# Spreading the cached keys and values of a small decode batch over the projection, gate and prompt-attention stages of a four-layer trunk

## The chip, the cores and the metric

The kernel runs on one core of a Trainium2 chip. The figure of merit is the device time of one execution in microseconds (us). A core has a matrix engine (PE, with its weight loads shown as PEld), a vector engine (DVE), a scalar engine (ACT), a general engine (POOL) and a queue engine (SP). They run their own instruction lists in order and wait for each other by semaphores. DMAs are issued from SP, ACT or POOL.

## The reference

Four layers of a decoder trunk are computed in one launch, for a prompt of 1024 tokens and for a sample group of 8 sequences with 4 new tokens each. The layers are a gated short convolution, an RG-LRU block, differential attention, and the convolution again. Only the attention layer (the third) is touched here. Its parts, cut:

```python
def diff_attn_project(u, w_in, pos):
    q, k, v, z = jnp.split(u @ w_in, [QK_WIDTH, 2 * QK_WIDTH, 2 * QK_WIDTH + V_WIDTH], axis=-1)
    q = rope_partial(q.reshape(bsz, t, 2 * N_HEADS, HEAD_DIM), pos) * (HEAD_DIM ** -0.5)
    k = rope_partial(k.reshape(bsz, t, 2 * N_HEADS, HEAD_DIM), pos)
...
def diff_attn_prompt(q, k, v, lam):            # per block of 128 queries, causal
        sc = jnp.einsum('bqhd,bkhd->bhqk', qi, k).astype(jnp.float32)
        w = diff_combine(jax.nn.softmax(sc, axis=-1), lam)      # p[head, 0] - lam * p[head, 1]
        return jnp.einsum('bhqk,bkhd->bqhd', w, v)
...
def diff_attn_sample(q, k_new, v_new, cache_k, cache_v, page_table, lam):
    k_past = cache_k[page_table].reshape(bsz, -1, 2 * N_HEADS, HEAD_DIM)
    v_past = cache_v[page_table].reshape(bsz, -1, N_HEADS, V_HEAD_DIM)
    ...                                        # softmax over 2048 past and 4 new keys, then w @ v
def diff_attn_output(o, z, subln_g, lam_init, w_out):
    return (rms_norm(o) * subln_g * (1.0 - lam_init) * jax.nn.silu(z)) @ w_out
```

D_MODEL is 1024, there are 8 heads with two score maps each, a page holds 128 positions, and each of the 8 sequences has 16 pages of past keys and 16 of past values, 512 KB each. So 67 MB of keys and 67 MB of values are read.

## The kernel before

All work is float32; the larger products split an operand into a high and a low part (type float32r) and add the partial products. The attention layer has three stages for the prompt, and PE works through them in this order:

- **Projections** (`qkv`): 48 tiles (q, k and v in two halves each, 8 token tiles each), `qk<n>_<t>`, 24 matmuls each. Tiles of q and k are rotated on DVE, transposed on PE (`qkf`) and stored to DRAM.
- **Gate path** (`zpath`): 8 heads by 3 chunks, `zz<h>_<c>`, 24 matmuls each; tanh on ACT, product on DVE, stored to DRAM (`zd`) and read back in the next stage.
- **Heads** (`heads`): 8 heads by 8 query blocks: scores (`S`), row minima on DVE, exponentials on ACT (`P`), the difference of the two maps on DVE (line 1284), transposition on PE (`wtp`), copy on ACT, product with the values (`pv`). Keys and queries of a head come from DRAM (`kd`, `qd`) into tiles `tok` and are split into the high and low parts `ks` and `qhl`.

Two streams of work for the sample group are threaded into these stages. **Sample keys**: for each sequence and each of two feature halves, 16 half pages (`kp`, 256 KB each, issued from POOL, six buffers) are transposed on DVE into one tile `kt` with a single buffer (line 1476), and 64 groups of small matmuls (`sps`, line 1420, each shown as two records) multiply them by the queries. The document calls these sixteen pieces *halves* and the matmuls of one half a *burst*. After the second half come softmax, `spn` (new keys) and `spt` (transposition), and a store to DRAM (`psd`). **Sample values**: 128 whole pages (`vp`, issued from SP) are multiplied by these weights (`sacc`, line 1524). Keys hold a PSUM area that the values need in part, so all keys come before any value.

How much of a stream stands beside which stage is set by `merge`: as the prompt's stage yields pieces of nominal cost, a debt grows, and the side stream is written out until the debt is paid. The shares are in `self.shares` and `self.ahead`; `rest` writes out what is left. Before, the shares 0.76 and 0.26 put the keys beside the projections and the gate path, and all values stand beside the heads. A scheduler then moves instructions by its own model, mostly within a small distance; the order on each engine is fixed when the program is built.

The tiles `raw` (two buffers) take the raw weights of the gate path and the tiles `tok`. The tiles `zt` of the gate path have two buffers, and each is free again when its store has landed.

## Time and profile before

| what | us |
|---|---|
| median of 3 runs (lowest, highest) | 2407.51 (2405.63, 2414.55) |
| the profiled execution's own time | 2409.33 |
| its span, first to last instruction | 2407.7 |
| projections, 948 to 1350 | 402 |
| gate path, 1350 to 1486 | 136 |
| heads and values, 1486 to 1850 | 364 |

The three stages are 902 us of the span; the layers before and after them are not touched. The stage borders are where the first `qk`, `zz` and `S` matmul start and where the output projection takes over. "Busy" is the time in which an engine had an instruction under way. PE's matmuls overlap, so that an isolated group of them shows a longer busy time than the same group in a dense run.

### The profile page before, as it was taken

Reading aid. Unit: us, or ns where it says so; the run is one execution under the profiler, and the core shown is the slowest. Engines: PE = TensorE matmul, PEld = TensorE weight load, DVE = VectorE, ACT = ScalarE, POOL = GpSimd, SP = SyncE. Lnnn points to the kernel's source line nnn. Section 1 sums busy time; section 2 is a strip of 40 time slices with the busy share of each in tenths; the row PEclk is TensorE's granted clock in tenths of the full one; section 3 lists DMA queues with packets and bytes.
Section 4 is the critical chain, followed back from the end, with each engine's and each line's share of the span. In section 5 each row is a group of like instructions: output and inputs, shape, how many; then the busy total and the mean of one; then the engine's idle time right before and its main releaser. Section 6 shows DMA issues by size and latency. Waiting matters only on the chain.

```text
span 2407.7 us, 45325 instructions
## 1 busy us (share of the span) xinstructions
PE 2277.3 (95%) x17288; PEld 1946.8 (81%) x17288; DVE 1453.2 (60%) x3015; ACT 929.2 (39%) x1906; POOL 337.1 (14%) x541
## 2 busy tenths in 40 slices
PE   7999999999999999988999998888888999999997
PEld 4989999997888886766666886555557999999997
DVE  6865655457456545656555554677675477666555
ACT  4333333346544423322221113667665243333410
POOL 0200000001001000233223322333220000000000
PEclk9999999999999999999999998999999999999999
DMA  9243344423444535768677766999993222222442
GB/s 329 77 145 111 91 121 150 133 82 120 139 131 124 154 108 171 217 201 255 222 242 253 244 189 203 277 298 291 281 299 116 84 85 62 68 59 70 128 131 76
DMA packets 289391, 393.41 MB, mean 163 GB/s; under 512 B 18749, under 2 KB 197054, under 8 KB 289174
## 3 DMA queue, kind: packets, MB, share of 16 engines
q1 hardware_dynamic: 247190, 306.61, 42.1%
q0 software_dynamic: 20480, 67.13, 9.1%
q10 hardware_dynamic: 21504, 16.78, 2.1%
q8 instruction: 136, 2.23, 0.4%
q14 instruction: 81, 0.66, 0.1%
HBM read 331.14 MB, written 59.31 MB: 162 GB/s over the span
## 4 chain that ended last, share of the span: by engine, by line
PE 64%; issue 13%; DMA 11%; POOLq 5%; POOL 2%; DVE 2%; ACT 1%; SPq 1%; DVEq 0%; ACTq 0%
PE op L127 15%; PE inX L612 12%; PE inZ L612 6%; DMA vp<-cache_v 6%; PE xb L127 4%; PE z L127 4%; POOLq L1381 4%; PE in L127 3%; PE inY L612 3%; PE ada L200 3%; PE in L733 2%; PE in L648 2%; PE g L903 2%; POOL kp L1388 2%; PE sacc L1524 1%
## 5 line engine op out<-in xcount | busy, mean ns | idle before, releaser
L1099 PE MATMUL qk<-wq,ua 128*128 128x512 f32 x1152 | 284.1, 401 | 8.7 <-DVE wq L1067 5.5
L1099 PEld LDWEIGHTS qk<-wq,ua 128*128 128x128 f32 x1152 | 213.2, 189 | 68.4 <-DVE wq L1067 8.1
L1476 DVE STREAM_TRANSPOSE kt<-kp 128x512 f32<-128x512 f32 x256 | 172.0, 697 | 138.5 <-DMA kp<-cache_k 107.1
L1388 POOL DMA_DIRECT2D kp<-cache_k x256 | 137.9, 539 | 336.1 <-DVE kt L1476 188.8
L294 DVE SCALAR_TENSOR_TENSOR r<-op,gate,xr 128x384 f32<-128x384 f32 (+1 forms) x96 | 54.2, 570 | 127.4 <-PE op L127 82.5
L1262 ACT ACTIVATE P<-S,rr 128x512 f32<-128x512 f32 (+2 forms) x192 | 110.8, 583 | 47.1 <-DVE rr L1250 31.5
L1210 PE MATMUL S<-ks,qhl 128*128 128x512 f32 (+2 forms) x384 | 110.8, 395 | 13.8 <-ACT P L1262 7.4
L127 PE MATMUL zz<-ua,wz 128*128 128x384 f32 (+1 forms) x576 | 99.0, 331 | 7.0 <-DVE zt L1165 7.0
L1210 PEld LDWEIGHTS S<-ks,qhl 128*128 128x128 f32 x384 | 60.8, 196 | 54.8 <-ACT P L1262 30.7
L127 PEld LDWEIGHTS zz<-ua,wz 128*128 128x128 f32 x576 | 95.6, 193 | 11.4 <-DVE zt L1165 7.8
L127 PEld LDWEIGHTS z<-ub,wrz 128*128 128x128 f32 x576 | 92.6, 188 | 11.7 <-issue 10.1
L1524 PE MATMUL sacc<-vp,pv 128*16 128x256 f32 x1024 | 80.3, 389 | 22.9 <-DMA vp<-cache_v 22.7
L127 PE MATMUL z<-ub,wrz 128*128 128x384 f32 (+1 forms) x576 | 98.2, 326 | 0.0
L1303 PEld LDWEIGHTS pv<-V,wt 128*128 128x128 f32 x576 | 73.7, 194 | 22.5 <-ACT wt L1295 13.4
L127 PEld LDWEIGHTS xb<-ub,wrx 128*128 128x128 f32 x504 | 80.9, 188 | 12.7 <-issue 9.2
L1420 PE MATMUL sps<-kt,qbd 32*32 32x512 f32 x2048 | 78.8, 621 | 11.9 <-DVE kt L1476 11.9
L331 POOL TENSOR_TENSOR rs<-mv,mhalf 128x1 f32<-128x1 f32 (+1 forms) x36 | 19.1, 541 | 504.3 <-DVE mv L329 497.6
L127 PE MATMUL op<-ua,ub 128*128 128x384 f32 (+1 forms) x504 | 89.7, 333 | 0.0
L127 PEld LDWEIGHTS op<-ua,ub 128*128 128x128 f32 x504 | 81.9, 192 | 9.1 <-issue 9.0
L127 PE MATMUL xb<-ub,wrx 128*128 128x384 f32 (+1 forms) x504 | 87.9, 328 | 0.0
L1303 PE MATMUL pv<-V,wt 128*128 128x128 f32 x576 | 82.3, 284 | 5.8 <-ACT wt L1295 5.3
L200 PE MATMUL ada<-wada,ct 128*32 128x512 f32 x384 | 82.7, 616 | 4.1 <-DMA wada<-w_ada 2.9
(492 smaller groups left out, 5112.4 us busy)
## 6 DMA issues: line engine op xcount, KB each, us to landing
kp<-cache_k POOLq DMA_DIRECT2D x256, 256.0 KB, 3.8
vp<-cache_v SPq DMA_DIRECT2D x128, 512.0 KB, 10.0
wada<-w_ada SPq DMA_DIRECT2D x96, 512.0 KB, 4.2
xa<-xat SPq DMA_DIRECT2D x64, 192.0 KB, 2.6
wra<-a_w_in SPq DMA_DIRECT2D x24, 512.0 KB, 4.1
wrb<-a_w_in SPq DMA_DIRECT2D x24, 512.0 KB, 4.1
xr<-xa SPq DMA_DIRECT2D x64, 192.0 KB, 2.5
tok<-kd SPq DMA_DIRECT2D x32, 256.0 KB, 7.0
```

The source lines that it names most:

```text
L127: nc.tensor.matmul(ps[:, :n], wt[:, wp, k], self.ucols(units[k], up, c), start=i == 0, stop=i == 3 * KB - 1)
L200: nc.tensor.matmul(ps[c : c + 32, :], self.ct[:, k], wts[k // 2][:, k % 2], start=k < 4, stop=k >= 4, tile_position=(0, c),)
L612: nc.tensor.matmul(B[tgt][jj][:, :QH], w[n][:, wp, k], mov[k](jj, up), start=new and m == 0, stop=m == 11, skip_group_check=not new)
L1099: nc.tensor.matmul(ps, u[k][:, c0 : c0 + 128], wq[n, k // 2][:, wp, k % 2], start=i == 0, stop=i == 3 * KB - 1)
L1210: nc.tensor.matmul(st[:, o : o + w], qs[h, g][:, part, s, 128 * qj : 128 * qj + 128], ks[h][:, s, l0 : l0 + w], start=part == 0, stop=part ...
L1262: nc.scalar.activation(p[:, o : o + w], x["S"][s][i][:, :w], AF.Exp, scale=-1.0, bias=rr[:, 6 + s : 7 + s], accum_out=rr[:, c : c + 1])
L1303: nc.tensor.matmul(x["pv"], x["w"][kb // 4][:, j : j + 128], V[h][:, kb], start=kb == 0, stop=kb == qb)
L1381: ld, (r,) = nc.values_load_multi_w_load_instructions(self.ptab[0:1, idx : idx + 1], engines=[et], min_val=0, max_val=159)
L1388: d = eng.dma_start(t, a[src].rearrange(pat)[bass.ds(r, 1), :, cs].rearrange("a p f -> p (a f)"))
L1420: nc.tensor.matmul(ps[b][32 * g : 32 * g + 32, r], qf[rows, f, g, k], kt[rows, g, k], start=f == 0 and k == 0, stop=f == 1 and k == 3, til ...
L1476: nc.vector.transpose(ktv[:, :, j], ring.pop(0).rearrange("p (f t) -> p f t", t=32))
L1524: nc.tensor.matmul(acc[32 * g : 32 * g + 16, :], pt[:k, j, g], vv[:k, :, g], start=j == 0, stop=j == NPG, tile_position=(0, 32 * g))
```

## The change

The merging shares become 0.98 and 0.4 (the latter over two chunks of the gate path only, then the rest of the keys is written out), so that all keys stand beside the projections and the first gate chunks. The sample values begin right after, at 0.3 of their nominal cost over the gate path, and the remaining 0.7 beside the heads; their pages get seven buffers instead of five. The stores of the gate path move from SP's queue to ACT's, one chunk late: the store of a chunk is issued behind the tanh of the next. Keys and queries of the prompt heads are fetched once, 256 KB by one DMA where two DMAs of 256 KB each were, with 128 partitions of 512 instead of 128 of 2 by 512; the copies to the other half of the partitions are made on the core. For keys, ACT makes two copies of 64x512 instead of one of 128x1024, and POOL subtracts as before, two times 64x512. For queries, ACT makes two copies of 64x512, DVE two further copies of 64x512 (new), and POOL four subtractions of 64x512 instead of one of 128x1024. Lines behind the edits move by up to 8.

```diff
--- before.py
+++ after.py
@@ -1150,6 +1150,7 @@
             return self.load_w(wv[:, :, c : c + 128], f"wz{h}")
 
         wt = ld(0)
+        late = []
         for h in range(KB):
             nxt = ld(h + 1) if h < KB - 1 else None
             for c in range(3):
@@ -1158,14 +1159,17 @@
                 ps = self.gemm_chunk(wt, u, c, f"zz{h}_{c}")
                 t = self.sm(f"zt{h}_{c}")
                 nc.scalar.activation(t[:, :n], ps[:, :n], AF.Tanh, scale=0.5)
+                if late:
+                    nc.scalar.dma_start(*late.pop())
                 if npr < n:
                     nc.vector.scalar_tensor_tensor(
                         self.szs[:, h], t[:, npr:n], 1.0, ps[:, npr:n], ALU.add, ALU.mult
                     )
                 nc.vector.scalar_tensor_tensor(t[:, :npr], t[:, :npr], 1.0, ps[:, :npr], ALU.add, ALU.mult)
-                nc.sync.dma_start(self.zd[h][:, c0 : c0 + npr], t[:, :npr])
+                late.append((self.zd[h][:, c0 : c0 + npr], t[:, :npr]))
                 yield 10.2 * n
             wt = nxt
+        nc.scalar.dma_start(*late.pop())
 
 
     def heads(self, y):
@@ -1176,11 +1180,10 @@
         ks, V, sz, qs, O, ss = {}, {}, {}, {}, {}, {}
 
 
-        def twice(q, h, g):
-            t = self.raw([128, 2, 512], f"tok{q}{h}_{g}")
-            src = self.qkT[q][128 * h : 128 * h + 128, 512 * g : 512 * g + 512]
-            for rows in halves[0]:
-                nc.sync.dma_start(t[rows], src.rearrange("(s p) f -> p s f", p=64))
+
+        def fetch(q, h, g):
+            t = self.raw([128, 512], f"tok{q}{h}_{g}")
+            nc.sync.dma_start(t, self.qkT[q][128 * h : 128 * h + 128, 512 * g : 512 * g + 512])
             return t
 
         def keys(h, g):
@@ -1190,18 +1193,22 @@
                 nc.sync.dma_start(
                     V[h], self.vd[:, 128 * h : 128 * h + 128].rearrange("(j p) f -> p j f", p=128)
                 )
-            t = twice(1, h, g)
+            t = fetch(1, h, g)
             cs = slice(512 * g, 512 * g + 512)
-            nc.scalar.copy(ks[h][:, :, cs], t)
             for s, (own, oth) in enumerate(halves):
-                lo = ks[h][oth, s, cs]
-                nc.gpsimd.tensor_tensor(lo, t[oth, s], lo.bitcast(F32), ALU.subtract)
+                hi = ks[h][own, s, cs]
+                nc.scalar.copy(hi, t[own])
+                nc.gpsimd.tensor_tensor(ks[h][oth, s, cs], t[own], hi.bitcast(F32), ALU.subtract)
 
         def queries(h, g):
-            t = twice(0, h, g)
+            t = fetch(0, h, g)
             qhl = self.wtile([128, 2, 2, 512], F32R, f"qhl{h}_{g}")
-            nc.scalar.copy(qhl[:, 0], t)
-            nc.gpsimd.tensor_tensor(qhl[:, 1], t, qhl.bitcast(F32)[:, 0], ALU.subtract)
+            for s, (own, oth) in enumerate(halves):
+                hi = qhl[own, 0, s]
+                nc.scalar.copy(hi, t[own])
+                nc.vector.tensor_copy(qhl[oth, 0, s], t[own])
+                for rows in (own, oth):
+                    nc.gpsimd.tensor_tensor(qhl[rows, 1, s], t[own], hi.bitcast(F32), ALU.subtract)
             qs[h, g] = qhl
 
         def product(st, h, qb, s, o, l0, w):
@@ -1589,18 +1596,19 @@
         cq.__exit__(None, None, None)
         ct, self.tmp = self.pool("tmpq", reuse_waits="tile")
         z, ztot = self.zpath(u), 8 * 10.2 * NT
-        merge(itertools.islice(z, 20), ztot, keys, self.shares[1] * KEY_COST)
-
+        merge(itertools.islice(z, 2), ztot, keys, self.shares[1] * KEY_COST)
+        rest(keys)
+
+        self.deal(tp="QU", tps="P", mm="R")
+        values = self.sample_values(u)
+        next(values)
+        merge(itertools.islice(z, 18), ztot, values, self.zshare * VALUE_COST)
         cpa, self.ppa = self.pool("ppa", reuse_waits="tile")
         hs = self.heads(u)
         next(hs)
-        merge(z, ztot, keys, self.shares[1] * KEY_COST)
-        rest(keys)
+        merge(z, ztot, values, self.zshare * VALUE_COST)
         ca, self.pp = self.pool("pp", reuse_waits="tile")
-        self.deal(tp="QU", tps="P", mm="R")
         tot = 64 * 9 * 110.0 + 288 * 324.0 + 16 * 430
-        values = self.sample_values(u)
-        next(values)
 
         def main():
             while True:
@@ -1610,7 +1618,7 @@
                     break
                 yield c
 
-        merge(main(), tot, values, VALUE_COST * self.ahead)
+        merge(main(), tot, values, VALUE_COST * (1 - self.zshare) * self.ahead)
         rest(values)
         ca.__exit__(None, None, None)
         cpa.__exit__(None, None, None)
@@ -1730,7 +1738,7 @@
                 cm.__exit__(None, None, None)
             self.bufs = dict(sm=2)
             self.n_sz, self.n_ks, self.n_p, self.n_tok, self.n_wt, self.n_o = 1, 2, 4, 2, 3, 2
-            self.shares, self.ahead, self.n_vp = (0.76, 0.26), 1.1, 5
+            self.shares, self.zshare, self.ahead, self.n_vp = (0.98, 0.4), 0.3, 1.1, 7
             cc, cp = self.pool("acst", reuse_waits="tile", side="right")
             cr, self.ropep = self.pool("ropep", reuse_waits="tile", side="right")
             self.attn_consts(cp)
```

On PE, in the projections: the burst of sequence 4's second half in the list before (`kt4_1` is its transposed key tile, `qk4_6` the seventh tile of the first half of the v projection):

```order
L1099 MATMUL qk4_6_14554<-wq4_3_13379,ua6_84 128x512 x3
L1099 MATMUL qk4_6_14554<-wq4_3_13379,ua7_85 128x512 x3
L1420 MATMUL sps4_14179<-kt4_1_14278,qbd_9885 32x512 x64
L1429 MATMUL spn4_14647<-ksb_8495,qbd_9885 32x32 x32
L1099 MATMUL qk4_7_14691<-wq4_0_12890,ua0_78 128x512 x3
```

The same burst in the list of the change:

```order
L1099 MATMUL qk4_0_14636<-wq4_3_14010,ua7_85 128x512
L1436 MATMUL spn4_14365<-ksb_8495,qbd_9885 32x32 x6
L1427 MATMUL sps4_13892<-kt4_1_13957,qbd_9885 32x512 x64
L1436 MATMUL spn4_14365<-ksb_8495,qbd_9885 32x32 x26
L1099 MATMUL qk4_0_14636<-wq4_3_14010,ua7_85 128x512 x2
```

It stands some six projection tiles earlier. The last burst (sequence 7, second half) stood behind `zz6_1` and now stands behind `zz0_0`, with 23 gate chunks still to come.

On PE, in the gate path, at the end of chunk `zz1_2` in the list before:

```order
L127 MATMUL zz1_2_16149<-ua6_84,wz1_15715 128x288 x3
L127 MATMUL zz1_2_16149<-ua7_85,wz1_15715 128x288 x3
L127 MATMUL zz2_0_16249<-ua0_78,wz2_15981 128x384 x3
L127 MATMUL zz2_0_16249<-ua1_79,wz2_15981 128x384 x3
L127 MATMUL zz2_0_16249<-ua2_80,wz2_15981 128x384 x3
```

The same place in the list of the change (`vp0_1` is sequence 0's second page of values):

```order
L127 MATMUL zz1_2_17058<-ua6_84,wz1_16719 128x288 x3
L1531 MATMUL sacc0_16898<-vp0_0_16899,pv0_16862 16x256 x4
L127 MATMUL zz1_2_17058<-ua7_85,wz1_16719 128x288 x3
L127 MATMUL zz2_0_17109<-ua0_78,wz2_16931 128x384 x3
L127 MATMUL zz2_0_17109<-ua1_79,wz2_16931 128x384 x3
L127 MATMUL zz2_0_17109<-ua2_80,wz2_16931 128x384 x3
L1531 MATMUL sacc0_16898<-vp0_1_16915,pv0_16862 16x256 x4
```

From here to the end of the gate path stand the products of 32 cached pages and of the new tokens of sequences 0 and 1, 34 in all, where before there was none; before, the first of them stood among the heads.

On DVE, in the heads, around the difference of the two maps of head 0, block 3 (line 1284 before, 1291 after; `rr` holds the row sums) in the list before:

```order
L1281 RECIPROCAL rr0_3_17696<-rr0_3_17696 128x2
L1282 SCALAR_TENSOR_TENSOR rr0_3_17696<-rr0_3_17696,nlam_5858 128x1
L1284 SCALAR_TENSOR_TENSOR P0_3_0_17704<-P0_3_1_17755,rr0_3_17696,P0_3_0_17704 128x512
L1248 TENSOR_REDUCE rr0_4_17757<-S0_4_1_0_17772 128x1
L1250 ISA S0_4_1_1_17776,rr0_4_17757<-S0_4_1_1_17776,cmask_17569,rr0_4_17757 128x128
```

The same place in the list of the change:

```order
L1288 RECIPROCAL rr0_3_18268<-rr0_3_18268 128x2
L1209 CAST qhl1_0_18544<-tok01_0_18542 64x512 x2
L1289 SCALAR_TENSOR_TENSOR rr0_3_18268<-rr0_3_18268,nlam_5858 128x1
L1291 SCALAR_TENSOR_TENSOR P0_3_0_18276<-P0_3_1_18311,rr0_3_18268,P0_3_0_18276 128x512
L1255 TENSOR_REDUCE rr0_4_18313<-S0_4_1_0_18328 128x1
```

The two new copies of the queries of head 1 (they wait for the DMA that brings `tok`) stand in DVE's list in the middle of the softmax of a block of head 0.

## Rows read from the trace of the kernel before

**Rows 1.** The page, part 1: busy us (share of the span) xinstructions.
```profile
PE 2277.3 (95%) x17288; PEld 1946.8 (81%) x17288; DVE 1453.2 (60%) x3015; ACT 929.2 (39%) x1906; POOL 337.1 (14%) x541
```

**Rows 2.** Stages by windows: length, busy us by engine, clock, DMA share, GB/s.
```profile
core 0: us, PE busy (x) PEld busy (x) DVE busy (x) ACT busy (x) POOL busy (x), PEclk, DMA share, GB/s
948.00:1350.00 402.00, 375.12 (x3349) 270.37 (x3350) 221.92 (x459) 97.10 (x152) 112.52 (x209) 0.98 0.73 229
1350.00:1486.00 136.00, 124.58 (x1270) 112.51 (x1270) 67.91 (x125) 27.81 (x46) 38.87 (x62) 0.95 0.63 192
1486.00:1850.00 364.00, 306.55 (x2472) 201.59 (x2471) 255.59 (x661) 240.90 (x732) 102.87 (x73) 0.97 0.93 267
```

**Rows 3.** The chain that ended last, 1530 to 1790, by line.
```profile
by line: DMA vp<-cache_v 50.2%; DMA tok<-qd 8.3%; PE sacc L1524 8.0%; PE S L1210 6.5%; PE pv L1303 5.3%; issue 2.9%; DMA tok<-kd 2.7%; PE wtp L1293 2.6%; DVE os L1530 2.1%; DVE P L1284 1.8%; ACT P L1262 1.4%; DVE rr L1282 1.3%; SPq L1388 1.
```

**Rows 4.** PE's waits, 1490 to 1820: us in total, times, longest.
```profile
PE sacc L1524 <- DMA vp<-cache_v: 22.7, 27, 1.9
PE wtp L1293 <- DVE P L1284: 7.5, 8, 1.8
```

**Rows 5.** Timeline of POOL from 1258, two successive page issues: start us, us.
```profile
1259.77 0.54 POOL L1388 DMA_DIRECT2D kp<-cache_k  x1 [14.60 <-DVE kt L1476]
1261.13 0.54 POOL L1388 DMA_DIRECT2D kp<-cache_k  x1 [0.82 <-DVE kt L1476]
```

**Rows 6.** Timeline of DVE over the same half: start us, us, count, idle before.
```profile
1258.66 3.67 DVE L1476 STREAM_TRANSPOSE kt<-kp 128x512 f32<-128x512 f32 x6 [8.97 <-PE sps L1420]
1262.77 0.71 DVE L1476 STREAM_TRANSPOSE kt<-kp 128x512 f32<-128x512 f32 x1 [0.44 <-DMA kp<-cache_k]
...
1276.55 0.71 DVE L1476 STREAM_TRANSPOSE kt<-kp 128x512 f32<-128x512 f32 x1 [0.76 <-DMA kp<-cache_k]
1281.82 2.29 DVE L1434 TENSOR_REDUCE smx<-sps 128x1 f32<-128x2048 f32 x1 [4.55 <-PE sps L1420]
```

**Rows 7.** Timeline of PE, the burst of the same half.
```profile
1277.32 4.03 PE L1420 MATMUL sps<-kt,qbd 32*32 32x512 f32 x114 [0.81 <-DVE kt L1476]
```

**Rows 8.** Line 1476 in 983 to 1145.5: min/median/max ns, first and last start.
```profile
L1476 DVE STREAM_TRANSPOSE kt<-kp x96: 668/711/715, 983.9 to 1144.4; 128x512 f32<-128x512 f32 x96
```

**Rows 9.** Groups of 948 to 1350: busy us, mean ns, idle before.
```profile
L1476 DVE STREAM_TRANSPOSE kt<-kp 128x512 f32<-128x512 f32 x201 | 135.1, 698 | 107.6 <-DMA kp<-cache_k 78.1 <-PE sps L1420 28.9
L1420 PE MATMUL sps<-kt,qbd 32*32 32x512 f32 x1536 | 61.0, 629 | 11.9 <-DVE kt L1476 11.9
```

**Rows 10.** Groups of 1350 to 1486, PE.
```profile
L127 PE MATMUL zz<-ua,wz 128*128 128x384 f32 (+1 forms) x576 | 99.0, 331 | 7.0 <-DVE zt L1165 7.0
L1420 PE MATMUL sps<-kt,qbd 32*32 32x512 f32 x512 | 17.8, 597 | 0.0
L1451 PE MATMUL spt<-ident,sc 128*128 128x128 f32 x48 | 7.5, 324 | 4.4 <-ACT sc L1439 4.4
```

**Rows 11.** Waits of ACT, 1350 to 1486.
```profile
ACT zt L1160 <- DMA zd<-zt: 37.9, 6, 11.5
```

**Rows 12.** The group of the value products, 1486 to 1850.
```profile
L1524 PE MATMUL sacc<-vp,pv 128*16 128x256 f32 x1024 | 80.3, 389 | 22.9 <-DMA vp<-cache_v 22.7
```

**Rows 13.** DMAs of 1486 to 1850: packets; issues by line, KB, us to landing.
```profile
DMA packets 41675, 97.18 MB, mean 267 GB/s; under 512 B 4032, under 2 KB 15168, under 8 KB 41635
vp<-cache_v SPq DMA_DIRECT2D x128, 512.0 KB, 10.0
tok<-qd SPq DMA_DIRECT2D x28, 256.0 KB, 11.5
tok<-kd SPq DMA_DIRECT2D x25, 256.0 KB, 7.4
```

**Rows 14.** Two windows of 30 us in the heads, columns as in rows 2.
```profile
1610.00:1640.00 30.00, 27.15 (x246) 17.55 (x238) 24.20 (x64) 21.09 (x65) 10.27 (x8) 1.00 0.99 299
1790.00:1820.00 30.00, 28.36 (x260) 17.87 (x260) 24.14 (x70) 21.23 (x71) 4.49 (x5) 1.00 0.69 238
```

**Rows 15.** Line 1284 in the third head (first row) and the last.
```profile
L1284 DVE SCALAR_TENSOR_TENSOR P<-P,rr,P x8: 343/810/1284, 1582.6 to 1621.3; 128x128 f32<-128x128 f32 x1, 128x256 f32<-128x256 f32 x1, 128x384 f32<-128x384 f32 x1, 128x512 f32<-128x512 f32 x1
L1284 DVE SCALAR_TENSOR_TENSOR P<-P,rr,P x8: 354/818/1279, 1796.5 to 1835.7; 128x128 f32<-128x128 f32 x1, 128x256 f32<-128x256 f32 x1, 128x384 f32<-128x384 f32 x1, 128x512 f32<-128x512 f32 x1
```

**Rows 16.** Two DVE lines, whole run: min/median/max ns, first and last start.
```profile
L1282 DVE SCALAR_TENSOR_TENSOR rr<-rr,nlam x64: 199/220/2152, 1493.8 to 1835.3; 128x1 f32<-128x1 f32 x64
L1455 DVE COPY sc<-spt x8: 1184/1222/1225, 1063.9 to 1481.0; 128x1024 f32<-128x1024 f32 x8
```

**Rows 17.** Groups of 1486 to 1850: DVE, then POOL.
```profile
L1282 DVE SCALAR_TENSOR_TENSOR rr<-rr,nlam 128x1 f32<-128x1 f32 x64 | 23.1, 362 | 2.2
...
L1204 POOL TENSOR_TENSOR qhl<-tok,qhl 128x1024 fp32r<-128x1024 f32 x15 | 35.7, 2380 | 114.4 <-ACT qhl L1203 90.3 <-DMA vp<-cache_v 19.8 <-PE pv L1303 4.2
L1198 POOL TENSOR_TENSOR ks<-tok,ks 64x512 fp32r<-64x512 f32 x26 | 34.0, 1309 | 41.4 <-ACT ks L1195 39.9
```

## The prediction

> **What bounds the kernel now.** Over the whole span PE is busy for 95% [rows 1], which says little: the three stages of the attention layer have different limits, so I read the windows of the stages first [rows 2], then the chain of waits inside a stage, then the groups and timelines that give unit prices. In the projections and the gate path PE idles for 27 and 11 us of 402 and 136. In the heads it idles for 57 of 364 us, and there the DMA share is 0.93 over the stage and 0.99 inside it [rows 2, 14]. The chain that ended last shows what the heads wait for: half of it is the transfer of value pages and another 11% the transfers of keys and queries [rows 3]. So the heads are bound by DMA: 97.18 MB in 364 us [rows 13], at a share that leaves no room. PE itself shows only 22.7 us of waits for pages [rows 4], because PE, DVE and ACT go on with queued blocks.
>
> The second thing to see is how the sample keys run. While the tile `kt` has one buffer, a half is a serial loop: transpose 16 half pages, burst, transpose again. POOL issues a page every 1261.13 - 1259.77 = 1.36 us [rows 5]. In the half shown, DVE does six waiting pages at once and then waits for POOL's pages one by one, from 1258.66 to 1276.55 + 0.71 = 1277.26, that is 18.6 us [rows 6]. The burst starts 0.06 us later [rows 7] and is over at 1281.8, when the reduction starts: 4.5 us. After every second half the reduction of 2.29 us stands ahead of the next transposition [rows 6]. That is (2 x 23.2 + 2.3) / 2 = 24.3 us a half as the floor, whatever PE does.
>
> **The change part by part.** All sums are against the profiled execution (2409.33 us; span 2407.7), which lies 1.8 us above the median of 2407.51.
>
> *Keys into the projections.* Before, 201 of 256 half pages were transposed by 1350, with 12 of 16 bursts [rows 9]. Now 15 bursts lie in the projections and the last behind the first gate chunk. PE's own work up to there is 375.1 us of before [rows 2], four more bursts of 4.5, a gate chunk of 99.0 / 24 = 4.1 [rows 10] and some 6 for softmax and transposition of two more sequences: 403 us. With the 15 us of idle time that have nothing to do with keys (27 less 11.9 [rows 9]) PE would be there at 948 + 418 = 1366. But the loop of keys starts at 983.9 [rows 8] and has 16 halves. At the floor it ends at 983.9 + 16 x 24.3 = 1373. From the first 96 pages, six halves that ran nearly without slack, the pace is (1144.4 - 983.9 - 18) / 5 = 28.5 [rows 8], which would give 1440; there several bursts had pieces of projection tiles between their matmuls. In the new order only about one burst in four is broken in that way, so I take a value nearer to the floor, 25.9: the last burst ends at 983.9 + 16 x 25.9 = 1398. PE then stalls before most bursts, two or three us each, 32 us beyond what it must do. I found no cover for this: the list has nothing else for PE to do at these places but what stands behind the burst.
>
> *Gate path.* After the last burst 23 chunks remain, 23 x 4.1 = 95 us. To this come 3 us for the last sequence's softmax and 34 value products (32 pages and two groups of new tokens). A product is 80.3 / 128 = 0.63 us of busy time [rows 12]; in dense work it will be a little less, say 0.6: 20 us. The gate stores on ACT's queue take away the waits that show as 37.9 us on ACT [rows 11] and 7.0 on PE [rows 10], which I have left out above; so I put no stall here. The pages need 17 MB in about 98 us, with 8 MB of weights, stores and reads beside them: 255 GB/s, below the 299 seen [rows 14], so the transfers keep up, without much to spare. The gate path ends at 1398 + 118 = 1516, against 1486.
>
> *Heads.* 32 of the 128 pages are gone, and two are as good as there (17.8 MB), and of the 53 fetches of keys and queries, 256 KB each, half (7 MB) [rows 13]: 97.2 - 17.8 - 7 = 72 MB, at the 299 GB/s of the full window [rows 14] 242 us. DMA no longer binds. What binds next is not shown by any row directly, so I bound it from both sides. *PE*: 306.6 us busy less 34 x 0.6 = 286; where pages had nearly run out, 1790 to 1820, PE was busy for 28.36 of 30 us [rows 14]. 286 / 0.945 = 303, and about 12 for the first fill and the drain: 315. *DVE*: 255.6 us busy [rows 2], and the change adds to it. The 30 copies of 64x512 in this stage have no row; the nearest is 128x1024 in 1.22 us [rows 16], so 0.6 each, 18 us. In that same late window DVE was busy for 24.14 of 30 us, 0.805. Line 1282, which works on one column, takes 0.22 us at the median and 2.15 at most [rows 16], 362 ns on the mean over 64 [rows 17]: it is held up while POOL subtracts. That is 9 us on this line alone, some 20 with the larger lines beside it, against 86 us of POOL's data work. For queries POOL will need 4 x 1.31 instead of 2.38 us [rows 17], 43 us more in the stage, so some 10 us more of such holds. (255.6 + 18 + 10) / 0.805 = 352. Between 315 and 352 I take 335. The last head speaks against the low end: its transfers had already thinned out (a share of 0.69 [rows 14]), yet its eight blocks took 39.2 us from first to last, as against 38.7 in a head amid full DMA [rows 15].
>
> The Trainium skill bears on these holds (page "SBUF — State Buffer", section "Who interferes with whom"): a VectorE instruction with two SBUF inputs contends with a GpSimd instruction that reads SBUF, and whichever starts first holds the port for its whole length. The maxima of line 1282 agree in size, up to one subtraction of 2.38 us. The same section has float32 copies from SBUF to SBUF hold that port too; by it each new copy could also wait for a subtraction that is under way, which is the fourth case below.
>
> *The rest.* ACT makes two copies of 64x512 where one of 128x1024 was, the same number of elements one after the other, and issues the gate stores; I cost both at nothing, since ACT is busy for 27.8 of 136 and 240.9 of 364 us [rows 2]. If ACT is held up by a store that waits for DVE, a tanh is late by that much, with three PSUM banks of slack on PE.
>
> Sum: 1398 + 118 + 335 = 1851, against 1850. The 57 us that the heads had idle are partly won (29 us), and lost again where the keys are pressed into a stage that is too short for their loop (48 us later at the end of the keys' part, of which 18 us come back in the gate path). The forecast is no change that can be measured: 2409.33 + 1 = 2410 us. A measurement of this kernel can tell about 0.5%, 12 us, from no change.
>
> **The rivals.**
> *The heads follow PE.* If the blocks keep PE at 0.945 once pages are no longer late, the heads take 315 us: 1398 + 118 + 315 = 1831, 19 us faster, 2390. For it: the waits for pages are half of the chain [rows 3]. Against it: the last head [rows 15].
> *The keys' loop at its measured pace.* If halves take 28.5 instead of 25.9 us, the last burst ends at 1440 and all behind it is 42 us later: 2452. It decides from about 26.7 us a half (13 us later than I take). For it: that is what the first six halves did; against it: the half at 1258 ran at the floor [rows 6].
> *That the keys keep up*: at 24.3 us a half PE is the limit (1373) and the rest as above: 25 us earlier, 2385. It needs every half at its floor and I give it little.
> *DVE is held by POOL in the heads.* The two copies stand in the middle of the softmax of a block and wait there for the DMA of `tok`, with the difference of the maps queued behind them, and for POOL. At 352 us for the heads the sum is 1868, 18 us slower: 2427. It decides from about 347. For it: the holds already there [rows 16, 17]; against it: DVE is not on the chain for more than some 5% now [rows 3].
>
> **How the numbers follow.** No change 0.40; heads follow PE 0.24; keys keep up 0.08; keys' loop slower 0.12; DVE held 0.16. So faster by over 0.5% 0.32, within 0.5% 0.40, slower 0.28. Within the first case the time lies between 2398 and 2422. The range over cases reaches from 2376, where the heads follow PE and the keys are somewhat better than 25.9, to 2444, where DVE is held and the halves take 27: that leaves out about 2 in 10.
>
> **What would show it.** Right, if the last `sps` burst ends near 1398, with PE waits of `sps` for DVE `kt` at 30 to 50 us in the projections instead of 11.9; if the gate path ends near 1516 with no wait for `zt`; if the heads show a DMA share near 0.75, hardly a PE wait for `vp`, and last some 335 us. Wrong, if halves are 24 or 28 us apart; if `sacc` waits for pages in the gate path by more than 8 us, where I put none; if the two DVE copies of queries cost more than 0.6 us each or leave DVE waiting for `tok`; or if the heads fall below 315.

## The result, and the profile of the changed kernel

The changed kernel takes 2475.73 us (median of 4 runs, 2473.4 to 2481.08) against 2406.57 for the kernel before: a ratio of 1.028, with a 95% interval of 1.0244 to 1.0316. The forecast was no change, 2410 us in 2376 to 2444; the result lies outside, on the slow side. The profiled execution took 2481.08 us, its span is 2479.4 against 2407.7, so 71.7 us are to be found.

Part 1 of its page, as [rows 1]:

```profile
PE 2310.8 (93%) x17288; PEld 1964.6 (79%) x17288; DVE 1485.1 (60%) x3047; ACT 935.8 (38%) x1938; POOL 390.7 (16%) x589
```

PE's busy time grew by 33.5 us with the same 17288 instructions. So part of the loss is PE instructions that show longer, not only waits. The stages as windows, cut at the end of the last burst and of the gate path's matmuls, as the forecast counts them (the first gate chunk lies in the first window):

```profile
core 0: us, PE busy (x) PEld busy (x) DVE busy (x) ACT busy (x) POOL busy (x), PEclk, DMA share, GB/s
948.00:1440.00 492.00, 419.00 (x4048) 297.58 (x4047) 266.62 (x540) 102.72 (x162) 143.09 (x261) 0.93 0.72 223
1440.00:1555.00 115.00, 115.00 (x862) 95.59 (x854) 28.66 (x59) 23.21 (x40) 13.01 (x13) 1.00 0.78 268
1555.00:1920.00 365.00, 303.20 (x2192) 207.83 (x2192) 280.58 (x678) 246.63 (x760) 151.69 (x119) 0.92 0.54 182
```

The keys' part ends at 1440 where 1398 was forecast, the gate path takes 115 us (forecast 118), and the heads 365 (forecast 335). The first and the third are the miss: 42 + 30 us, less 3. The granted clock is 0.93 in the first window and 0.92 in the last, against 0.98 and 0.97 in [rows 2].

**The keys.** PE's longest wait from 948 to 1440 (us in total, times, longest), and the group of the bursts (busy us, mean ns, idle before):

```profile
PE sps L1427 <- DVE kt L1483: 28.3, 7, 7.1
```

```profile
L1427 PE MATMUL sps<-kt,qbd 32*32 32x512 f32 x2048 | 90.2, 734 | 45.1 <-DVE kt L1483 28.3 <-DVE qbd L1420 12.8 <-DVE sc L1463 2.0
```

The first row is the stall that the forecast wanted, 28.3 us where [rows 9] have 11.9; it is just under the 30 to 50 that were named. But bursts also waited for `qbd` (the queries) and for softmax work (`sc`) on DVE, 45.1 us with these. In all PE was idle for 73.0 of the 492 us, 26 more than the 47 (15 + 32) of the forecast, and busy for 419.0, 16 more than its 403: these are the 42 us. What makes work longer can be seen behind a stall. The last half on DVE (start, us, count, idle before it):

```profile
1411.95 3.68 DVE L1483 STREAM_TRANSPOSE kt<-kp 128x512 f32<-128x512 f32 x6 [4.64 <-PE sps L1427]
...
1428.61 0.71 DVE L1483 STREAM_TRANSPOSE kt<-kp 128x512 f32<-128x512 f32 x1 [2.25 <-DMA kp<-cache_k]
1430.88 0.71 DVE L1483 STREAM_TRANSPOSE kt<-kp 128x512 f32<-128x512 f32 x1 [1.56 <-DMA kp<-cache_k]
1433.23 0.71 DVE L1483 STREAM_TRANSPOSE kt<-kp 128x512 f32<-128x512 f32 x1 [1.64 <-DMA kp<-cache_k]
```

The burst behind it on PE:

```profile
1407.46 4.45 PE L1427 MATMUL sps<-kt,qbd 32*32 32x512 f32 x128 [2.41 <-DVE kt L1483]
...
1426.25 0.64 PE L1436 MATMUL spn<-ksb,qbd 32*32 32x32 f32 x50
1434.00 6.07 PE L1427 MATMUL sps<-kt,qbd 32*32 32x512 f32 x128 [7.11 <-DVE kt L1483]
```

Transposing took 22.0 us here (1411.95 to 1433.94; 18.6 in [rows 6]): the last three pages came 2.3 us apart, not 1.36. And the burst took 6.07 us where the one before it took 4.45. The clock around the two bursts, with the columns of the windows above:

```profile
1407.00:1412.20 5.20, 4.74 (x130) 2.50 (x131) 0.56 (x2) 0.00 (x0) 1.80 (x4) 1.00 0.99 340
1426.90:1430.60 3.70, 0.00 (x0) 0.00 (x0) 0.71 (x1) 0.00 (x0) 0.39 (x1) 1.00 0.99 293
1430.60:1434.00 3.40, 0.00 (x1) 0.01 (x1) 1.48 (x3) 0.00 (x0) 0.00 (x0) 0.50 1.10 309
1434.00:1437.40 3.40, 3.40 (x64) 1.21 (x65) 0.38 (x1) 0.00 (x0) 0.00 (x0) 0.50 0.20 70
1437.40:1440.00 2.60, 2.60 (x94) 1.84 (x77) 0.00 (x0) 0.00 (x0) 0.00 (x0) 0.99 0.02 6
```

PE had nothing to do from 1426.9 to 1434.0. In the second half of that pause the granted clock falls to 0.50, that is 1.2 of 2.4 GHz, and the burst's first 64 matmul records run at it for 3.4 us; its last 94 records, some of them the small `spn` matmuls, take 2.6 us at 0.99. Over all 16 halves the means are: transposition 19.8 us, burst 6.1, 2.4 between them, 28.3 together (986.7 to 1440.1). In [rows 6] and [rows 7] transposition and burst are 18.6 and 4.5. The excess of the bursts, 27 us in all, has two parts. Seven bursts stand behind a pause of 3 us or more, with only `spn` or a single projection matmul beside their own; they take 6.0 to 6.2 us, at a clock of 0.68 to 0.72 (11 us). Four have transpositions of projection tiles (`qkf`) between their matmuls; they take 6.1 to 10.2 us, at 0.79 to 0.83, and in the longest PE stands still for 3.65 us (15 us). The other five take 4.5 to 5.4. POOL's pages still start 1.35 us apart in the undisturbed stretch:

```profile
1415.80 0.56 POOL L1395 DMA_DIRECT2D kp<-cache_k  x1 [0.82 <-DVE kt L1483]
1417.15 0.55 POOL L1395 DMA_DIRECT2D kp<-cache_k  x1 [0.79 <-DVE kt L1483]
```

**The gate path.** Groups of PE, 1440 to 1556 (busy us, mean ns, idle before):

```profile
L127 PE MATMUL zz<-ua,wz 128*128 128x384 f32 (+1 forms) x552 | 96.9, 328 | 0.0
L1531 PE MATMUL sacc<-vp,pv 128*16 128x256 f32 x262 | 19.9, 383 | 0.0
```

PE is busy for all 115.0 us of this window. The 7.0 us that `zz` waited for `zt` in [rows 10] are gone, and nothing waits for value pages.

**The heads.** The two windows of [rows 14] again; they lie in the second and the sixth head now:

```profile
1610.00:1640.00 30.00, 27.72 (x245) 16.82 (x241) 23.72 (x54) 22.01 (x65) 13.13 (x12) 1.00 0.86 300
1790.00:1820.00 30.00, 24.71 (x117) 20.12 (x117) 23.21 (x66) 21.36 (x70) 12.06 (x10) 0.73 0.17 54
```

The DMA share is 0.86 and 0.17, in the mean over the stage 0.54 against 0.93. PE did not get busier for it: 24.71 of 30 us with hardly a transfer, at a clock of 0.73. Such a stretch has no value products, since these are all done 158 us before the stage ends (minimum, median, maximum ns; first and last start):

```profile
L1531 PE MATMUL sacc<-vp,pv x1024: 379/379/634, 1460.8 to 1760.9; 128*16 128x256 f32 x171
```

The chain of waits over a stretch of the heads like that of [rows 3]:

```profile
by line: PE S L1217 20.2%; PE pv L1310 13.6%; PE sacc L1531 11.8%; ACT P L1269 9.7%; PE wtp L1300 6.3%; DVE P L1291 5.8%; DVE S L1257 4.0%; issue 3.7%; DVE qhl L1209 2.9%; DVE rr L1289 2.3%; ACT qhl L1208 2.2%; DVE ua L1239 2.2%; ACT wt L13
```

The transfers of values, half of the chain before, are gone from it. In their place stand the pieces of a block's own softmax: scores `S`, exponentials and difference `P`, transposition, products `pv`. The waits of PE, 1560 to 1900, say the same (in [rows 4] the pages headed the list):

```profile
PE S L1217 <- ACT P L1269: 19.9, 29, 2.6
PE pv L1310 <- ACT wt L1302: 18.4, 19, 1.8
...
PE sacc L1531 <- DMA vp<-cache_v: 0.3, 1, 0.3
```

ACT's largest wait in the heads, first of the kernel before, then of the changed one; its releaser is the reduction of row minima on DVE:

```profile
ACT P L1262 <- DVE rr L1250: 31.5, 27, 3.8
```

```profile
ACT P L1269 <- DVE rr L1257: 52.9, 35, 5.0
```

And two DVE groups of that stage, to be set against 924 ns of busy time for the difference before (59.1 us for 64), and 0.6 us estimated for a copy:

```profile
L1291 DVE SCALAR_TENSOR_TENSOR P<-P,rr,P 128x128 f32<-128x128 f32 (+3 forms) x64 | 68.5, 1070 | 2.1
...
L1209 DVE CAST qhl<-tok 64x512 fp32r<-64x512 f32 x30 | 23.3, 776 | 1.1 <-PE S L1217 0.5
```

### The profile page after: what moved, and what is told of

Read it like the earlier page. It is cut to its first block, busy times and chain, and to the rows that moved or that the text cites. A ratio compares the mean times of both kernels' runs of the same rounds, so it can differ in the third digit from the quotient of the medians.

```text
span 2479.4 us, 45392 instructions
## 1 busy us (share of the span) xinstructions
PE 2310.8 (93%) x17288; PEld 1964.6 (79%) x17288; DVE 1485.1 (60%) x3047; ACT 935.8 (38%) x1938; POOL 390.7 (16%) x589
## 4 chain that ended last, share of the span: by engine, by line
PE 69%; issue 13%; POOLq 5%; DVE 4%; DMA 4%; ACT 3%; POOL 2%; SPq 0%; DVEq 0%; ACTq 0%
PE op L127 15%; PE inX L612 11%; PE inZ L612 6%; POOLq L1388 4%; PE xb L127 4%; PE zz L127 4%; PE z L127 4%; PE in L127 3%; PE inY L612 3%; PE S L1217 3%; PE ada L200 3%; PE sacc L1531 2%; PE in L733 2%; PE in L648 2%; PE g L903 2%
## 5 line engine op out<-in xcount | busy, mean ns | idle before, releaser
L1217 PE MATMUL S<-ks,qhl 128*128 128x512 f32 (+2 forms) x384 | 117.7, 416 | 20.5 <-ACT P L1269 19.9
L1269 ACT ACTIVATE P<-S,rr 128x512 f32<-128x512 f32 (+2 forms) x192 | 110.7, 581 | 63.7 <-DVE rr L1257 52.9
L1427 PE MATMUL sps<-kt,qbd 32*32 32x512 f32 x2048 | 90.2, 734 | 45.1 <-DVE kt L1483 28.3
L1427 PEld LDWEIGHTS sps<-kt,qbd 32*32 32x32 f32 x2048 | 36.9, 114 | 82.9 <-issue 34.3
L127 PEld LDWEIGHTS z<-ub,wrz 128*128 128x128 f32 x576 | 92.6, 188 | 11.7 <-issue 10.1
L1211 POOL TENSOR_TENSOR qhl<-tok,qhl 64x512 fp32r<-64x512 f32 x64 | 86.2, 1347 | 93.7 <-ACT qhl L1208 90.6
L667 POOL COPY psv<-cp 128x32 f32<-128x32 f32 x14 | 7.3, 523 | 520.5 <-DVE cp L678 482.5
```

Source lines behind the costliest of these rows:

```text
L127: nc.tensor.matmul(ps[:, :n], wt[:, wp, k], self.ucols(units[k], up, c), start=i == 0, stop=i == 3 * KB - 1)
L1211: nc.gpsimd.tensor_tensor(qhl[rows, 1, s], t[own], hi.bitcast(F32), ALU.subtract)
L1217: nc.tensor.matmul(st[:, o : o + w], qs[h, g][:, part, s, 128 * qj : 128 * qj + 128], ks[h][:, s, l0 : l0 + w], start=part == 0, stop=part ...
L1269: nc.scalar.activation(p[:, o : o + w], x["S"][s][i][:, :w], AF.Exp, scale=-1.0, bias=rr[:, 6 + s : 7 + s], accum_out=rr[:, c : c + 1])
L1427: nc.tensor.matmul(ps[b][32 * g : 32 * g + 32, r], qf[rows, f, g, k], kt[rows, g, k], start=f == 0 and k == 0, stop=f == 1 and k == 3, til ...
```

## The experiments

"Front" means the time to the end of the gate path's matmuls, "heads" what follows until the output projection starts. In the profiled executions of the kernel before and of the changed kernel these are 1486.2 and 362.1, and 1555.1 and 364.7. Ratios are against the kernel before on the same chip, with 95% intervals. Spans are of single profiled executions; the kernel before alone ran between 2393 and 2423 us on one chip, so a difference of a few us between two spans is not read. The profiled execution lay up to 11 us off its kernel's median (9: 2406.65 for 2395.67), fronts in which nothing was edited ended between 1475.6 (5) and 1492.2 (9), and the same heads took 364.7 us in the changed kernel and 373.1 in 2: differences of up to some 10 us between fronts or heads are no more than this scatter. A single head is counted from one head's last difference of the maps (line 1284) to the next one's.

**1. Keys early, no values beside the gate path.** Edit to the changed kernel:

```
-  self.shares, self.zshare, self.ahead, self.n_vp = (0.98, 0.4), 0.3, 1.1, 7
+  self.shares, self.zshare, self.ahead, self.n_vp = (0.98, 0.4), 0.0, 1.1, 7
```

> The change with no values beside the gate path (their share there 0 instead of 0.3; all else as in the change). Theory K (the serial loop of the keys' halves is what costs the time in front of the gate path): the last burst ends near 1440 us as in the change (28 us a half), the gate path takes some 95 us more, and the heads, with all 136 value products, some 365 to 375 us; 2455 to 2475 us in all. Rival V (the values beside the gate path disturb more than they help): the loss goes, near 2410 us.

Measured: 2472.54 us, ratio 1.0247 [1.0199, 1.0295]. The gate path's matmuls (first and last start in the line):

```profile
L127 PE MATMUL zz<-ua,wz x576: 290/334/441, 1417.2 to 1527.7; 128*128 128x384 f32 x128, 128*128 128x288 f32 x64
```

Front 1528.0, heads 385.1. So the keys alone cost the front 41.8 us, the values beside the gate path another 27.1, and they relieve the heads of 20.4 (I had expected heads of 365 to 375). The last burst ended at 1436.9: the keys' pace has nothing to do with the value pages.

**2. Two issuers for key pages.** Edit to the changed kernel: every second key page is issued from SP (shortened).

```
-  (nc.sync, SP, "P") if half is None else (nc.gpsimd, Pool, "H"))
+  (nc.sync, SP, "P") if half is None
+  else (nc.gpsimd, Pool, "H") if idx % 2 == 0 else (nc.sync, SP, "P"))
```

> The change with every second key page issued from SP instead of POOL; the order on PE is the same. Theory K with POOL's 1.36 us a page as the loop's pace: the transposition of a half falls from 19.8 us (mean in the change) to about 15, a half from 28.4 to some 23, the last burst ends near 1370 to 1380, and the run is 50 to 65 us faster than the change, near 2415 us. Rival D (transfers or DVE set the pace of a half, not the issue): a half stays above 27 us and the time within 15 us of the change.

Measured: 2439.24, ratio 1.0111 [1.0061, 1.016]. A half on DVE:

```profile
1264.79 3.67 DVE L1484 STREAM_TRANSPOSE kt<-kp 128x512 f32<-128x512 f32 x6 [7.95 <-PE sps L1428]
...
1277.65 1.30 DVE L1484 STREAM_TRANSPOSE kt<-kp 128x512 f32<-128x512 f32 x2 [3.48 <-DMA kp<-cache_k]
1279.25 1.31 DVE L1484 STREAM_TRANSPOSE kt<-kp 128x512 f32<-128x512 f32 x2 [0.30 <-DMA kp<-cache_k]
```

It takes 15.8 us, and pages now come in pairs. Over 16 halves transposition takes 16.0, a burst 5.0, all together 25.1 (983.0 to 1385.3). The last burst ends 54.8 us earlier than in the changed kernel and the front is 51.6 us shorter, 8.4 of which the heads give back. So the issue interval on POOL was the root of the keys' loss. Bursts got shorter too, when nothing but the supply of pages was changed: three of 16 ran at a lowered clock (0.72 to 0.76), where the changed kernel has twelve. The run is 36.5 us faster, not the 50 to 65 expected. Even with the loop repaired the change is slower than before: the heads lose as well.

**3. Value products spread over all heads.** Edit to the changed kernel: each product is tied, in PE's order, behind the score matmul that was issued before it (13 to 15 products in each of heads 0 to 6 and 7 in the last; in the changed kernel 20 to 24 in heads 0 to 3, none in the last three).

```
+  self.lead = nc.tensor.matmul(st[:, o : o + w], ...)
...
+  mm = nc.tensor.matmul(acc[32 * g : 32 * g + 16, :], pt[:k, j, g], ...)
+  if g == 0 and self.lead is not None:
+      self.after(mm, self.lead)
```

> The change with each value product tied, in PE's order alone, behind the score product written before it, so that 13 to 15 products stand in each head instead of 20 to 24 in the first four and none in the last three. Theory H (values used up too early leave the last heads without filler): the heads go from 365 to about 340 us, 2450 us in all. Rival Q (the query copies hold DVE in the heads): the heads stay within 8 us of 365.

Measured: 2470.39, ratio 1.0233 [1.0184, 1.0282]. Heads 360.4, 4.3 us less. The uneven use of the pages is real, and I had not counted it, but it is worth almost nothing: what the early heads gain the last ones pay.

**4. Keys and queries fetched twice, as before.** Edit to the changed kernel, for both:

```
-  t = fetch(0, h, g)
+  t = twice(0, h, g)
...
-  for s, (own, oth) in enumerate(halves):
-      hi = qhl[own, 0, s]
-      nc.scalar.copy(hi, t[own])
-      nc.vector.tensor_copy(qhl[oth, 0, s], t[own])
-      for rows in (own, oth):
-          nc.gpsimd.tensor_tensor(qhl[rows, 1, s], t[own], hi.bitcast(F32), ALU.subtract)
+  nc.scalar.copy(qhl[:, 0], t)
+  nc.gpsimd.tensor_tensor(qhl[:, 1], t, qhl.bitcast(F32)[:, 0], ALU.subtract)
```

> The change with keys and queries fetched twice as before (ACT copy 128x1024, one POOL subtraction for queries, no DVE copy). Rival Q: the heads lose the 32 DVE copies and some 43 us of POOL's subtractions and become 15 to 25 us shorter, 2450 to 2460 us. Theory H: the heads change by less than 8 us, since chain and filler are as in the change; the time stays within 10 us of 2475.

Measured: 2469.85, ratio 1.0237 [1.0187, 1.0287]. Heads 354.6, 10.1 less, between the two expectations. ACT's waits in the heads:

```profile
ACT P L1267 <- DVE rr L1255: 31.4, 26, 4.2
ACT ks L1200 <- DMA tok<-kd: 23.6, 9, 8.9
```

The wait for row minima is back at what it was before the change, 31.4 us. But ACT now waits 23.6 us for the doubled transfers of keys: the single fetch of keys was worth something.

**5. The single fetch alone.** Edit to the kernel before: the reverse of 4.

> The kernel before with only the single fetch of keys and queries (two more ACT copies and two DVE copies of 64x512 for queries, four POOL subtractions). Front of the heads as before (last burst near 1468, gate path to 1486). Theory T (transfers bound the heads of before): 7 MB less at some 280 GB/s, the heads lose up to 20 us; 2385 to 2395 us. Rival Q (the copies and subtractions for queries hold DVE): what the transfers give is taken back, the heads are within 5 us of 362 or up to 10 us longer; 2402 to 2418 us.

Measured: 2427.99, ratio 1.0086 [1.0055, 1.0118]: slower by itself, beyond both expectations. Front 1475.6, though nothing in it was edited; heads 385.4, 23.3 more than before. Line 1204, the two copies of queries, over the whole run:

```profile
L1204 DVE CAST qhl<-tok x32: 421/1160/1453, 1462.6 to 1802.0; 64x512 fp32r<-64x512 f32 x32
```

A copy takes 421 ns when nothing disturbs it, and 1160 at the median here, 1453 at most. ACT's wait for row minima is 48.0 us (31.5 before).

**6 and 7. Fewer value pages.** Edits to the kernel before; 6 takes 12 of the 16 pages of each sequence, 7 takes one.

```
-  for j in range(NPG + 1):
+  for j in [*range(12), NPG]:
```

> The kernel before with 12 of 16 value pages of each sequence (32 of 128 pages are neither loaded nor multiplied). This is the change's relief of the heads with nothing else changed. The prediction's term (heads bound by transfers, 36.8 MB of relief would show nearly in full until PE or DVE binds): the heads go from 362 to about 335 us. Theory F (the products are filler in gaps of a softmax chain that takes some 38 us a head by itself, so a page costs 0.35 us there): 362 - 32 x 0.35 = 351 us. Also what 38 us a head says: no head falls under 37.

> The kernel before with 1 of 16 value pages of each sequence, all of them used up at the start of the heads, so that seven heads run with no value page at all. Theory F: they take 36 to 39 us each, the stage some 310 to 320 us. The prediction's term (PE at 0.945 of the time once no page is late): PE's own work without pages would be about 230 us, the stage some 255 us.

Measured: 6 took 2405.8, ratio 0.9992 [0.9974, 1.001], and 7 took 2398.4 in a single run. The heads of 6 as a window, and 200 us in the heads of 7:

```profile
1488.70:1844.00 355.30, 289.50 (x2210) 198.07 (x2208) 245.89 (x659) 240.94 (x732) 102.64 (x73) 0.95 0.79 226
```

```profile
1560.00:1760.00 200.00, 149.41 (x822) 116.18 (x822) 148.29 (x374) 147.09 (x451) 70.25 (x51) 0.91 0.29 78
```

With 32 pages less the DMA share of the heads falls from 0.93 to 0.79 and the heads gain 6.7 us (355.4). The pages are missing from the last two heads, which take 36.5 and 35.9 us instead of 44.1 and 41.8. The six others keep theirs: they take 4 us more in all, and PE still waits 18.1 us for pages there (22.7 before). The median fell by only 1.9 us, within its interval. With nearly all pages gone the share is 0.29. The first head, which has all the value products that are left, takes 60.5 us, the second 45.2, and the last six still 36 to 40, against 41.8 to 43.5 for five of them before and 44.1 for the sixth. The stage takes 348.2 us, not the 310 to 320 that I expected, since the first two heads were slow. What PE waits for there, until 1840:

```profile
PE S L1210 <- ACT P L1262: 40.6, 40, 1.7
PE wtp L1293 <- DVE P L1284: 13.8, 15, 2.7
PE pv L1303 <- ACT wt L1295: 10.2, 17, 1.2
```

No page is in the list. A head is a chain of scores, exponentials, difference, transposition and products, and 36 to 40 us is what this chain takes. That is some 5 us less than with 16 pages and the transfers at their limit, 0.3 us a page, where a value product keeps PE busy for 0.63 [rows 12]. So the value pages can have cost a head those 5 us of 43 at most, their products and their lateness together. The length of the stage does not follow from its bytes, though the DMA share was 0.99. Late transfers still had a price in it: 5 us a head would be some 40 over eight, and 8 shows a stage in which the pages are on time.

**8. The front repaired, keys early left out.** Edits to the kernel before: the two issuers of 2, the gate stores on ACT's queue issued one chunk later (as in the change), and keys, but not queries, fetched once.

```
+  if late:
+      nc.scalar.dma_start(*late.pop())
...
-  nc.sync.dma_start(self.zd[h][:, c0 : c0 + npr], t[:, :npr])
+  late.append((self.zd[h][:, c0 : c0 + npr], t[:, :npr]))
```

> The kernel before, shares and all, with three edits: every second key page issued from SP, the gate stores on ACT's queue one chunk late, and keys (not queries) fetched once. Theory K: faster halves take the waits for keys out of the projections (12 us) and the late stores the 7 us of waits in the gate path; 3.5 MB less in the heads is worth up to 10 us. 2380 to 2395 us. If issue and stores are not what PE waits for: within 5 us of 2406.

Measured: 2382.04, ratio 0.9878 [0.9843, 0.9914]: the fastest version, faster than both kernels. The time is in the expected range, but by luck: waits in the front were to give 19 us and keys once up to 10 in the heads, and the front is as before, 1485.3. Heads 338.5, as a window, and the chain over 1520 to 1770:

```profile
1485.30:1824.00 338.70, 304.57 (x2468) 198.45 (x2467) 248.34 (x661) 241.17 (x744) 105.20 (x76) 0.97 0.85 275
```

```profile
by line: PE S L1215 16.3%; PE pv L1308 13.8%; PE sacc L1530 13.6%; ACT P L1267 9.0%; PE wtp L1298 6.3%; DVE P L1289 5.0%; DMA vp<-cache_v 4.4%; issue 4.3%; DVE S L1255 4.1%; ACT ks L1202 3.6%; ACT wt L1300 3.3%; ACT qhl L1208 3.2%; DVE rr L
```

All of the gain lies in the heads, at a DMA share of 0.85. All pages are still read there, but they are 4.4% of the chain (50.2% in [rows 3]), PE waits 2.8 us for them (22.7 before), and a head takes 40.5 us in the mean, 2.4 more than the last six of 7, which have no page.

**9. Keys fetched once alone.** Edit to the kernel before: only the keys' part of the single fetch.

> The kernel before with only the keys (not the queries) of the prompt heads fetched once. Theory A (of the three edits of the repaired front, this one alone shortened the heads, since ACT no longer stands waiting for two transfers of a key tile amid full DMA): heads near 340 instead of 362 us, 2385 us in all. Rival B (the heads were shortened by something the other two edits do): heads within 6 us of 362.

Measured: 2395.67, ratio 0.9949 [0.9926, 0.9971]. Heads 354.2, 7.9 less than before, in a profiled execution that was the slowest of six. PE waits 12.8 us for pages. Experiment 5 differs from this by the single fetch of queries with its DVE copies, and its heads are 31.2 us longer. I had expected 9 to show nearly all of the gain of 8, and it does not; another 16 us in the heads of 8 come with the late stores, the two issuers or the order of instructions that results, and which of them was not settled.

**10. Keys early, everything else repaired.** Edits to the changed kernel: two issuers, queries fetched twice, no values beside the gate path, five value buffers as before.

> The change with every second key page issued from SP, the queries fetched twice as before (no DVE copy), five page buffers, and no values beside the gate path. Last burst near 1385, gate path to about 1480, heads as in the repaired front, some 340 us: 2380 us in all, within 8 us of the repaired front, whose gate path ended at 1485. If pressing the keys together costs PE time in itself, 2395 or more.

Measured: 2392.46, ratio 0.9945 [0.9928, 0.9962]. Last burst at 1392.1, front 1486.3, the same as before. With a half of 25.5 us the early keys cost the front nothing, and gain nothing either: what they take from the gate path they add to the projections. The time is 12 us above the 2380 expected and 10 above that of 8: the heads take 348.5 us, 10.0 more than in 8, with the same edits in them. Why was not settled.

**11. The same, with values beside the gate path** (share 0.3 instead of 0.0).

> As the kernel named e10_keys_early_repaired, but with 34 value products beside the gate path (share 0.3). Theory F (a product costs 0.6 us of dense PE time there and 0.1 to 0.35 us as filler in the heads): the gate path is 18 to 22 us longer, the heads 3 to 10 us shorter, so 8 to 19 us slower than that kernel. The prediction's term: the heads 25 us or more shorter, and the kernel some 5 to 10 us faster.

Measured: 2410.45, ratio 1.0026 [1.0012, 1.004]. The matmuls of the gate path in 10 and in 11:

```profile
L127 PE MATMUL zz<-ua,wz x576: 290/334/441, 1379.6 to 1486.0; 128*128 128x384 f32 x128, 128*128 128x288 f32 x64
```

```profile
L127 PE MATMUL zz<-ua,wz x576: 290/334/446, 1382.9 to 1510.0; 128*128 128x384 f32 x128, 128*128 128x288 f32 x64
```

The front is 24.0 us longer, 0.7 for each of 34 products; the heads are 7.8 us shorter (340.7), 0.23 for each. Moving a page out of the heads loses about 0.5 us, which the medians bear out: 11 is 18.0 us slower than 10.

**12. An intermediate share of early keys**, 0.86 in the place of 0.76, edit to 8.

```
-  self.shares, self.ahead, self.n_vp = (0.76, 0.26), 1.1, 5
+  self.shares, self.ahead, self.n_vp = (0.86, 0.16), 1.1, 5
```

> The repaired front (before with two issuers, late gate stores, keys once) with key shares 0.86 and 0.16: 14 bursts instead of 12 beside the projections. If two issuers leave the loop of the keys slack at this share, PE's work only moves: within 6 us of 2382. If PE already waits at this share, 10 us slower or more.

Measured: 2396.05, ratio 0.9956 [0.9939, 0.9974]. Front 1495.6, 10.3 longer than in 8; heads 335.8. I had expected it within 6 us of 8; it lost 14. The last burst stands at 1466.0 as in 8 (1467.4), with 29.6 us of gate path behind it instead of 17.9. Two bursts with projection pieces and pauses between their matmuls take 12.3 and 16.0 us, the others 4.5 to 7.1. The heads are 2.7 us shorter and the 10.3 of the front lie within the scatter of fronts, so where the 14 us went is not shown.

## Why the prediction was wrong

The 71.7 us, by fronts and heads: keys pressed together +41.8 (front of 1 less front before); values beside the gate path +27.1 in the front (changed kernel less 1) and -20.4 in the heads; the single fetch +23.0 in the heads (those of 1, 385.1, less before; 5 gives 23.3). Together 71.5. This holds because the runs share their fronts; that the single fetch is the 23.0 rests on 5. The parts in the heads are not independent: the same relief by fewer pages is 6.7 us in 6 and 7.8 in 11, where no queries are copied.

*"I take a value nearer to the floor, 25.9"* (keys' part, term mis-sized). The mechanism was right: the single `kt` makes the loop serial, and PE stalls before most bursts. The size was off: 28.3 a half, within 1% of the upper bound of 28.5, and the last burst ends at 1440.1, where the rival "The keys' loop at its measured pace" had it. A half is 4.0 us above the floor of 24.3, where I had allowed 1.6: the burst is 1.6 longer (6.1 for 4.5), the transposition 1.2 (19.8 for 18.6, with pages that came late), and 1.2 more lies between them. I had put the 28.5 of [rows 8] down to projection pieces between the matmuls. They are rarer in the changed kernel, four bursts of 16 as I had said, and hold 15 of the 27 us by which the bursts are too long; 11 more come behind pauses in which the clock fell. The floor came from one half in which PE had worked until 0.81 us before the burst [rows 7]; the change is made of halves where it often had not. A stall can have a price beyond its length, and I counted only the length; I also left out what a burst waits for besides `kt`, 16.8 of the 45.1 us.

*"So the heads are bound by DMA"* (the reading of the profile, wrong as I used it). From it I took 335 us, 27 less than the heads before, between a PE bound of 315 and a DVE bound of 352. The bounds excluded the truth, 364.7. The share of 0.99 and the chain of [rows 3] showed that transfers were always under way and came last at many places; they did not show what a head takes without them. Fewer transfers are worth 7 us for the pages (6, 11) and 8 for the keys (9), each within the scatter of spans (by the medians 2 for 6 and 10 for 9), 15 instead of 27. Experiments 8 and 12 gained 24 and 26 us in the heads with all pages left there, once the pages were on time. So 335 us is about what the heads take with transfers on time and no query copies; moving pages away is not what brings them there, and 16 of the 24 us in 8 remain unexplained. Both bounds took PE's or DVE's busy share of one window, where value products filled the gaps (0.945, 0.805), as the share that a stage without late pages would have; PE's share fell to 24.71 / 30 = 0.82. [Rows 15] had the warning: the last head took 39.2 us amid thin transfers, hardly more than one amid full DMA. I named it as speaking against the low end and did not let it set the term.

*"so 0.6 each, 18 us"* and "some 10 us more of such holds" (query copies, term put in the wrong place; the rival "DVE is held by POOL" was under-weighted). The work itself was sized well: DVE was busy for 25 us more (280.58 less 255.59), with 23.3 from the copies, at 776 ns each, 9.4 from the difference, at 1070 for 924 ns, and 8 less in the rest. But I put it into a bound on DVE's throughput, where it costs nothing until DVE is the limit. A copy stands in the middle of a block's softmax, with the row minima that ACT needs queued behind it: ACT's wait for them rose from 31.5 to 52.9 us and is 31.4 without the copies (4). Their price in the heads is 18 us in the changed kernel (10.1 in 4, to which the 7.9 of 9 are added, since 4 gives up the single fetch of keys too) and 31 in 5; 2 and 11, which differ by the fetch of queries and two page buffers, give 32 (373.1 less 340.7). With 18 the heads add up, 362.1 - 7 - 8 + 18 = 365, but the 8 of the keys stands in the 18 as well, so the sum only sets 4 beside 6 (354.6 and 355.4); the runs leave the price between 18 and some 32. That the copies wait for POOL can be read one by one. In the changed kernel the 19 copies that started with no POOL instruction under way took 419 to 424 ns; the 13 that started during one took 545 to 1399, and each ended 0.28 to 0.29 us after that instruction (rows below). The Trainium skill has the rule (page "SBUF — State Buffer", section "Who interferes with whom"): copies on VectorE (DVE) can take the ports that it shares with GpSimd (POOL), and whichever issues first holds them for its whole instruction. The trace agrees, by the 545 to 1399 ns above. No run held POOL off the copies, so how much of their price in the heads is this wait is not shown.

*Each rival alone.* Two rivals came true together, the keys' loop and the copies. I had priced them one by one, at 2452 and 2427; both at once are 2410 + 42 + 18 = 2470, near the 2475.73 measured, and no case held them both.

*Values beside the gate path.* Their price in the front was nearly right: 20 us forecast for 34 products, 23.9 measured (from the last burst to the end, 115.0 in the changed kernel and 91.1 in 1), and the gate path's 115 us as well. Wrong was the other side: in the dense gate path a product costs its full time, in the heads less than half of it when no copies disturb them.

*Right:* that about one burst in four is broken, no stall in the gate path, no wait for `zt`, a DMA share that falls in the heads (0.54, forecast 0.75: 66.61 MB in 365 us, where 72 in 335 were expected), page waits of PE gone (0.3 us for 22.7).

## What to carry to other kernels

A DMA share of 1 and a chain that ends in transfers say that transfers are late somewhere, not how long the stage would be without them; look for a stretch of the same work with thin transfers, or take the transfers out in a run, before moving work to make room. Filler work costs its full time in a dense stage and little in one that waits anyway, so it belongs where PE waits. And where a change makes a serial loop run without slack, price it by the halves that ran so already, not by the best one, and allow for what the clock can take after a stall. Rivals that can come true together need a case with both.
